# Residual sums by accumulating DMA, first squares on TensorE alone, and three smaller edits in a one-core streaming encoder layer

## The chip, the cores and the metric

The kernel runs on one core of a Trainium2 chip. The metric is the device time of one execution in microseconds (us). The engines are named as the profile names them: PE is TensorE (PEld its weight loads), DVE is VectorE, ACT is ScalarE, POOL is GpSimd, SP is SyncE, which here only issues DMAs.

## What is computed

One layer of a hybrid encoder, for 1024 prompt frames and 32 sample frames (T = 1056 tokens), with 1024 features and a feed-forward width of 2816, in float32:

```python
xn = rmsnorm(x, pre_mix_norm_w)
proj = xn @ w_in                                  # -> z | xbc | dt | u
y_ssd = ssd_mixer(z, xbc, dt_raw, ...)            # conv4, SiLU, chunked scan, 8 heads, gated norm
y_s5 = s5_mixer(u_s5, ...)                        # complex diagonal scan, GELU, GLU
mix = jnp.concatenate([y_ssd, y_s5], axis=-1) @ w_out
h = x + rmsnorm(mix, post_mix_norm_w)             # first residual sum
up, new_ffn = causal_dwconv(rmsnorm(h, pre_ffn_norm_w) @ w_up, ffn_hist, ffn_conv_w, ffn_conv_b)
gate, val = jnp.split(up, 2, axis=-1)
ffn = (jax.nn.gelu(gate, approximate=True) * val) @ w_down
y = h + rmsnorm(ffn, post_ffn_norm_w)             # second residual sum
```

## The kernel before

**Layout.** Everything is feature-major: 128 partitions by 8 feature blocks by tokens. The tokens are walked in three chunks, c0 of 512, c1 of 272 and c2 of 272 (block 0 is c0, block 1 is c1 and c2; the last 32 are the sample's). The matrix `o` (`O[b]`) holds the output projection and later h, `acc` (`ACC[b]`) the sum of the down projection.

**GEMMs.** Each product is three passes, high by high, low by high and high by low (L479). A weight tile `raw` of 512 KB is loaded by SP's DMA into a ring of two, its high part `wh` is copied by ACT (L535), its low part `wl` is subtracted by DVE (L713).

**Norms.** Squares (ACT) are added over pairs of feature blocks on POOL or DVE, a matmul with a column of ones (`ms<-onec`) brings the sum over features into a column, nine small DVE steps (L603 to L626) make 1/sqrt of it, `spread` puts the factors on a diagonal (`scr`, L646 and L647, or L639) and a matmul with ones spreads them over the partitions into PSUM (`ms<-scr,ones_r`). ACT then copies the factor to SBUF: `rbc` and `oacc` (r1 in the code), and `sacc` for the last norm.

**Stages in time.** Prologue (x loaded, split into `xh` by ACT and `xl` by DVE at L1045, squares, pair sums at L1029 on POOL); the input projections (u evacuated to `uext` at L758); the S5 scan and the SSD chunks beside them (masks `rh`, `rl` at L1349 on POOL, one pair for each SSD chunk); the output projection; `post` (from L1640), which scales `o` by r1 (L1659, DVE), adds x from the tile `xr` (L1660, POOL), splits h into `xh` and `xl`, adds its squares (L1666, POOL) and stores block 0's h to DRAM (`hd`, SP); the feed-forward blocks; `fin_out` and `apply`, which scale `acc` by the last factor (L1891, DVE or POOL by a table), add h (L1893, or L1896 from the reloaded `hr`) and store y (L1897, SP).

**What sets the order.** The side streams (S5, SSD, post, fin) are generators that are woven into the main GEMM stream. A planner then reads all instructions, finds their dependencies, prices each with a cost table (`cost`), makes a list schedule with a forward and a backward pass, and pins the order of every engine's queue. So an edit anywhere in the program, or in the table, can move instructions everywhere.

The two lines of `flush` on which the second edit turns:

```python
if k in (par["pairs"] if c == 0 else par["pairs2"]):
    G.tensor_tensor(a[-1], a[-1], r, add)
```

Of the kernel before, what the change touches and what calls it, by code (L numbers as in the profile page):

```python
# [9 lines left out]
F32 = mybir.dt.float32  # L10
# [9 lines left out]
WA = 512  # L20
# [161 lines left out]
class Plan:  # L182
# [61 lines left out]
    def read(self):  # L244
# [97 lines left out]
    def cost(self, q, i, ia, oa):  # L342
# [30 lines left out]
    def schedule(self, rank, pre, suc, forward=True, gate=None):  # L373
# [12 lines left out]
        while todo:  # L386
# [28 lines left out]
            if self.bytes[q]:  # L415
                if forward:
# [3 lines left out]
                end[q] = max(s + self.lat[q], wire + 0.8)  # L420
                lanes = lanes[1:] + [end[q]]
# [37 lines left out]
def body(tc, xT, wt, wdt, vec, cst, dtp, hist4, hist3, h0ssd, s5p, s5bc, s5d, glu, glub,  # L459
# [289 lines left out]
    h_dram = dram.tile([128, KD, WA], F32, name="hd")  # L749
# [591 lines left out]
    def ssd_front(c):  # L1341
# [301 lines left out]
    def post(b):  # L1643
        HN[b] = xtiles(b)
        for c in BLKC[b]:
# [7 lines left out]
            for j in range(4):  # L1653
                xr = iot("xr")[:, :, :w]
                D.dma_start(xr, xT[:, 2 * j:2 * j + 2, t0:t0 + w])
                for kk in range(2):
                    k = 2 * j + kk
                    h = O[b][:, k, o:o + w]
                    V.scalar_tensor_tensor(h, h, vc("post_mix", k), r1, mult, mult)  # L1659
                    (V if k in par["hv"] else G).tensor_tensor(h, h, xr[:, kk], add)  # L1660
# [9 lines left out]
                if b == 0:  # L1670
                    D.dma_start(h_dram[:, 2 * j:2 * j + 2], O[b][:, 2 * j:2 * j + 2, o:o + w])
# [188 lines left out]
    def fin_out(c):  # L1860
# [4 lines left out]
        r = fin[c][0]  # L1865
# [8 lines left out]
        if c == 1:  # L1874
            ap = [(1, j) for j in par["fp"][1]] + [(1, j) for j in range(4) if j not in par["fp"][1]][:par["ia"]]
        elif c == 2:
            ap = [(1, j) for j in range(4) if j not in par["fp"][1]][par["ia"]:] + ap
        with ExitStack() as es:
            if c == 2:
                es.enter_context(tc.issue_after(last[0].ins))  # L1880
            for c_, j in ap:
                apply(c_, j)
                yield 0.9

    def apply(c, j):
# [13 lines left out]
    hrs = {}  # L1899

    def fin_block(b):
        if b == 0:
            for j, n in enumerate(("ext0", "ext1", "W0", "G0", "T0", "C0")):
                h = tl(n, [128, 2 if j < 2 else 1, 512], "hr")
                k = 2 * j if j < 2 else j + 2
                D.dma_start(h, h_dram[:, k:k + h.shape[1]])
                for i in range(h.shape[1]):
                    hrs[k + i] = h[:, i]
# [37 lines left out]
```

## Time and profile before

| | us |
|---|---|
| median of three runs | 1296.92 |
| lowest and highest | 1296.79, 1300.04 |
| the profiled execution | 1294.34 |
| its span in the trace | 1292.4 |
| mean granted TensorE clock | 0.979 of 2.4 GHz |

The span is what the trace covers, from the first to the last recorded event; 1.94 us of the profiled execution lie outside it. The median lies 2.58 us above the profiled execution. Rows show a start and a length in us; an entry in brackets is the idle time of that engine before the row and what ended it. In rows by window the figure behind a busy time is the number of instructions.

### The profile page before, as it was taken

To read this page: it belongs to the slowest core of one execution; us is meant where nothing else is said; L and a number is where in the kernel's file an instruction comes from. 1 tells how busy PE (TensorE), PEld (TensorE's weight loads), DVE (VectorE), ACT (ScalarE), POOL (GpSimd) and SP (SyncE) were. 2 spreads that over 40 slices of the span, in tenths; PEclk is the share of its full clock that TensorE was granted. 3 is DMA by queue.
4 is the path that set the end of the run, shared out by engine and by line. 5 is a ranking of instruction groups with operands and counts; after the bars stand their busy time and mean duration, and the time that the engine had idled before them with its cause. 6 is when DMAs were issued, how large, how long until landed. Compare 5 with 4: busy or idle time off the path is not lost.

```text
span 1292.4 us, 20981 instructions
## 1 busy us (share of the span) xinstructions
PE 1225.8 (95%) x7880; PEld 1105.6 (86%) x7880; DVE 1035.2 (80%) x1781; ACT 574.5 (44%) x979; POOL 397.7 (31%) x577
## 2 busy tenths in 40 slices
PE   6879999999998999999999999998999999999995
PEld 5768888888877888878977888887999999999994
DVE  7898887988988998987688977679577777777777
ACT  7236466554555555543444433353523333333243
POOL 5364554544146433211345110015111111111113
PEclk8989999999998999999999999999999999999997
DMA  7133323233434423234433333222323332222212
GB/s 220 57 96 99 96 76 114 79 106 93 124 105 164 152 91 99 81 104 137 153 99 123 122 99 98 95 85 82 117 81 98 99 98 82 95 86 83 82 52 70
DMA packets 66901, 132.14 MB, mean 102 GB/s; under 512 B 13936, under 2 KB 34800, under 8 KB 66800
## 3 DMA queue, kind: packets, MB, share of 16 engines
q1 hardware_dynamic: 66800, 130.81, 32.2%
q8 instruction: 62, 1.02, 0.3%
q14 instruction: 39, 0.32, 0.1%
HBM read 111.69 MB, written 15.81 MB: 99 GB/s over the span
## 4 chain that ended last, share of the span: by engine, by line
PE 79%; DVE 10%; POOL 3%; issue 3%; DMA 2%; ACT 1%; SPq 1%; DVEq 0%; ACTq 0%; POOLq 0%
PE pm L479 70%; PE ms L479 9%; DVE wl L713 1%; POOL pacc L1666 1%; POOL o L1660 1%; DVE o L1659 1%; SPq L1122 1%; DMA xst<-xT 1%; DVE scr L647 1%; DVE scr L646 1%; POOL oacc L1628 1%; PE ms L483 1%; DVE pq L996 1%; POOL hq L1164 0%; DVE yr L1104 0%
## 5 line engine op out<-in xcount | busy, mean ns | idle before, releaser
L479 PE MATMUL pm<-xh,wh 128*128 128x272 f32 (+1 forms) x1616 | 532.1, 330 | 15.9 <-ACT wh L535 8.7
L479 PE MATMUL pm<-xh,wl 128*128 128x272 f32 (+1 forms) x1616 | 531.1, 329 | 7.4 <-DVE wl L713 7.3
L479 PE MATMUL pm<-xl,wh 128*128 128x272 f32 (+1 forms) x1616 | 529.8, 328 | 1.7 <-DVE xl L1045 1.7
L479 PEld LDWEIGHTS pm<-xh,wh 128*128 128x128 f32 x1616 | 309.9, 192 | 37.8 <-ACT wh L535 8.7
L479 PEld LDWEIGHTS pm<-xh,wl 128*128 128x128 f32 x1616 | 309.0, 191 | 30.8 <-DVE wl L713 9.1
L479 PEld LDWEIGHTS pm<-xl,wh 128*128 128x128 f32 x1616 | 309.9, 192 | 24.4 <-DVE xl L1045 3.0
L535 ACT ACTIVATE wh<-raw 128x1024 fp32r<-128x1024 f32 x120 | 126.9, 1057 | 177.5 <-PE pm L479 109.5
L713 DVE TENSOR_TENSOR wl<-raw,wh 128x1024 fp32r<-128x1024 f32 x120 | 154.9, 1291 | 26.6 <-ACT wh L535 26.1
L479 PE MATMUL pm<-al,dh 128*128 128x272 f32 (+1 forms) x528 | 171.4, 325 | 0.6 <-DVE al L1751 0.6
L479 PE MATMUL pm<-ah,dh 128*128 128x272 f32 (+1 forms) x528 | 171.7, 325 | 0.3 <-ACT ah L535 0.3
L479 PE MATMUL pm<-ah,dl 128*128 128x272 f32 (+1 forms) x528 | 170.8, 324 | 0.0
L1793 DVE TENSOR_TENSOR acc<-acc,pm 128x272 f32<-128x272 f32 (+1 forms) x235 | 121.1, 520 | 53.6 <-PE pm L479 52.5
L1738 DVE SCALAR_TENSOR_TENSOR ftmp<-fext,vec_t,ftmp 128x512 f32<-128x512 f32 (+1 forms) x176 | 143.1, 814 | 3.9 <-ACT ftmp L535 2.1
L1716 POOL COPY fext<-halo 128x2 f32<-128x2 f32 x88 | 33.6, 382 | 293.0 <-DVE ftmp L1738 271.5
L1721 DVE TENSOR_TENSOR fext<-pm,rbc 128x512 f32<-128x512 f32 (+2 forms) x132 | 67.5, 511 | 69.2 <-PE pm L479 65.8
L479 PEld LDWEIGHTS pm<-ah,dh 128*128 128x128 f32 x528 | 99.4, 188 | 8.6 <-ACT ah L535 0.7
L479 PEld LDWEIGHTS pm<-al,dh 128*128 128x128 f32 x528 | 99.3, 188 | 8.1 <-DVE al L1751 0.9
L479 PEld LDWEIGHTS pm<-ah,dl 128*128 128x128 f32 x528 | 99.2, 188 | 7.7 <-issue 0.3
L535 ACT ACTIVATE dh<-raw 128x1024 fp32r<-128x1024 f32 (+1 forms) x46 | 46.7, 1018 | 108.3 <-PE pm L479 96.8
L535 ACT ACTIVATE ftmp<-fext,vec_t 128x512 f32<-128x512 f32 (+1 forms) x88 | 72.3, 822 | 11.1 <-DVE fext L1721 5.7
L535 ACT ACTIVATE ftmp<-ftmp 128x512 f32<-128x512 f32 (+1 forms) x44 | 28.4, 644 | 87.0 <-DVE ftmp L1738 87.0
L1771 DVE TENSOR_TENSOR dl<-raw,dh 128x1024 fp32r<-128x1024 f32 (+1 forms) x46 | 55.9, 1216 | 13.6 <-ACT dh L535 13.6
(318 smaller groups left out, 1668.7 us busy)
## 6 DMA issues: line engine op xcount, KB each, us to landing
raw<-wt SPq DMA_DIRECT2D x164, 512.0 KB, 3.3
gluw<-glu SPq DMA_DIRECT2D x8, 512.0 KB, 3.4
xst<-xT SPq DMA_DIRECT2D x16, 136.0 KB, 3.3
pbd<-pbo SPq DMA_DIRECT2D x8, 272.0 KB, 2.6
xr<-xT SPq DMA_DIRECT2D x8, 272.0 KB, 3.2
pbi<-pbd SPq DMA_DIRECT2D x8, 272.0 KB, 3.5
yT<-acc SPq DMA_DIRECT2D x8, 272.0 KB, 2.3
ud<-uext SPq DMA_DIRECT2D x4, 528.0 KB, 4.0
```

What stands on the lines that cost most here:

```text
L479: PE.matmul(out, lhsT, rhs, start=start, stop=stop, **kw)
L483: PE.transpose(out, in_, ident)
L535: S.activation(out, in_, func, bias=bias, scale=scale)
L646: e.tensor_scalar(hi[:L, o:o + L], ident[:L, :L], r[:L, i:i + 1], None, mult)
L647: last[0] = V.scalar_tensor_tensor(lo[:L, o:o + L], ident[:L, :L], r[:L, i:i + 1], hi[:L, o:o + L].bitcast(F32), mult, sub)
L713: V.tensor_tensor(lo, r, hi.bitcast(F32), sub)
L996: V.tensor_scalar(pq[lo:hi, a], src[lo:hi, :, o:o + 8], sg, None, mult)
L1716: G.tensor_copy(e[:, 0:2], halo[:, j, :])
L1721: V.tensor_tensor(e[:, 2 + o:2 + o + wp], ps[:, :wp], rbc[:, t0:t0 + wp], mult)
L1738: V.scalar_tensor_tensor(t, e[:, i:i + n], vc("fw", 3 * j + i), t, mult, add)
L1771: V.tensor_tensor(l, rr, h.bitcast(F32), sub)
L1793: V.tensor_tensor(a, a, ps[:, :w], add)
```

## The change

Five edits, and a sixth in the planner's table.

1. **Residuals.** In `post`, x is no longer loaded into `xr` and added by POOL. POOL's queue issues a DMA from x in DRAM onto `o` that adds (`accum_op=add`), one for each two feature blocks. h is stored straight into the output `yT` by SP, for all chunks; `hd` and its reloads `hr` are gone. In `apply`, DVE alone multiplies, and POOL's queue issues a DMA that adds `acc` onto `yT` in DRAM. There are 12 + 12 such DMAs; 24 + 14 POOL steps, and the DVE steps L1893 and L1896, leave.
2. **First squares.** `pairs=()`: the five POOL sums of chunk 0's squares leave, and TensorE sums all eight (32 instead of 12 matmuls of one column before the factor of chunk 0).
3. **Masks.** Each SSD chunk's two POOL steps of 128x1024 with two tensor inputs become sixteen of 128x128 with one tensor input and a column as scalar.
4. **Last factor.** The ACT copy of the last factor to `sacc` is dropped; the multiplication reads PSUM.
5. **u.** `uext` is written in its own storage order, and PSUM and `rbc` are read with a stride, instead of the other way round.
6. **Planner.** POOL's DMAs are priced at 1.0 us of POOL and 3.5 us until landing, a GEMM matmul slightly differently, and two readers of a PSUM tile on one engine keep their order.

```diff
-pairs=(1, 2, 3, 5, 6)
+pairs=()
-            self.dur[q], self.lat[q] = 0.06, 2.0
+            self.dur[q], self.lat[q] = (0.06, 2.0) if e == "SP" else (1.0, 3.5)
-                d = max(0.43 * n + 6, 107 if m > 64 else 54)
+                d = max(0.426 * n + 9, 107 if m > 64 else 54)
...
-        V.tensor_tensor(ext4[j][:, :, n0:n1].rearrange("p s n -> p n s"),
-                        ps[:, :w].rearrange("p (n s) -> p n s", s=8),
-                        rbc[:, t0:t0 + w].rearrange("p (n s) -> p n s", s=8), mult)
+        V.tensor_tensor(ext4[j][:, :, n0:n1], ps[:, :w].rearrange("p (n s) -> p s n", s=8),
+                        rbc[:, t0:t0 + w].rearrange("p (n s) -> p s n", s=8), mult)
...
-            G.tensor_tensor(dst, src[:L, c].bitcast(F32)[:, :, None].to_broadcast([L, 8, L]), ub, mult)
+            for h in range(8):
+                G.tensor_scalar(dst[:, h, :], upper[:L, :L], src[:L, c, h:h + 1].bitcast(F32), None, mult)
...
-                D.dma_start(xr, xT[:, 2 * j:2 * j + 2, t0:t0 + w])
+                for kk in range(2):
+                    h = O[b][:, 2 * j + kk, o:o + w]
+                    V.scalar_tensor_tensor(h, h, vc("post_mix", 2 * j + kk), r1, mult, mult)
+                G.dma_start(O[b][:, 2 * j:2 * j + 2, o:o + w], xT[:, 2 * j:2 * j + 2, t0:t0 + w], accum_op=add)
...
-                    V.scalar_tensor_tensor(h, h, vc("post_mix", k), r1, mult, mult)
-                    (V if k in par["hv"] else G).tensor_tensor(h, h, xr[:, kk], add)
...
-                if b == 0:
-                    D.dma_start(h_dram[:, 2 * j:2 * j + 2], O[b][:, 2 * j:2 * j + 2, o:o + w])
+                D.dma_start(yT[:, 2 * j:2 * j + 2, t0:t0 + w], O[b][:, 2 * j:2 * j + 2, o:o + w])
...
-            act(r, norm_r(fin[c], w, scrt(*(("xo", "Z0"), ("xo", "W1"), ("T1", "G1"))[c]), G if c in par["fg"] else None, f"f{c}"),
-                AF.Copy)
+            fin[c] = [norm_r(fin[c], w, scrt(*(("xo", "Z0"), ("xo", "W1"), ("T1", "G1"))[c]), None, f"f{c}")]
...
-        e = G if j in par["fp"][c] else V
-        e.tensor_tensor(a, a, fin[c][0][:, None, :].to_broadcast([128, 2, w]), mult)
-        if b:
-            e.tensor_tensor(a, a, O[b][:, 2 * j:2 * j + 2, o:o + w], add)
-        else:
-            for kk in range(2):
-                e.tensor_tensor(a[:, kk], a[:, kk], hrs[2 * j + kk], add)
-        D.dma_start(yT[:, 2 * j:2 * j + 2, t0:t0 + w], a)
+        V.tensor_tensor(a, a, fin[c][0][:, None, :].to_broadcast([128, 2, w]), mult)
+        G.dma_start(yT[:, 2 * j:2 * j + 2, t0:t0 + w], a, accum_op=add)
```

**PE at the program's start.** `xh_111` and `xl_112` are the high and low part of chunk 0's x, `xh_165` and `xl_166` those of c1; `xst` is a tile of x that now holds its squares. Before, in the middle of the first GEMM rows:

```order
L479 MATMUL pm<-xh_111,wh 128x512
L479 MATMUL ms_295<-onec,xst 128x1
L479 MATMUL pm<-xh_165,wh 128x272
L479 MATMUL pm<-xl_112,wh 128x512
L479 MATMUL pm<-xh_111,wl 128x512
L479 MATMUL pm<-xl_166,wh 128x272
L479 MATMUL pm<-xh_165,wl 128x272
L479 MATMUL pm<-xh_165,wh 128x272
L479 MATMUL ms_295<-onec,xst 128x1 x11
```

After, from the first row of PE's queue:

```order
L1917 UNCONDITIONAL_BRANCH
L482 MATMUL ms_289<-onec,xst 128x1 x32
L482 MATMUL pm<-xh_110,wh 128x512
L482 MATMUL pm<-xl_111,wh 128x512
L482 MATMUL pm<-xh_110,wl 128x512
```

All sums of chunk 0's squares moved ahead of the first GEMM matmul; before, 22 GEMM matmuls stood ahead of the first of them. Ahead of the spread of chunk 0's factor (`ms<-scr,ones_r 128x512`) there stood 26 GEMM matmuls of 512 columns and 50 of 272, and now the 26 alone.

**POOL in post of block 0.** `o_3883` and `o_3953` are h of block 0, `pacc` the sum of its squares, `rh` and `rl` the masks of SSD chunks in work. Before:

```order
L1628 TENSOR_TENSOR oacc<-oacc,osq 128x512 x3
L1349 TENSOR_TENSOR rl_4719<-dtal,cst_t 128x1024
L1660 TENSOR_TENSOR o_3883<-o_3883,xr 128x512 x4
L1666 TENSOR_TENSOR pacc<-pacc,xr 128x512 x2
L1660 TENSOR_TENSOR o_3883<-o_3883,xr 128x512 x2
L1666 TENSOR_TENSOR pacc<-pacc,xr 128x512 x2
L1660 TENSOR_TENSOR o_3883<-o_3883,xr 128x512 x2
L1666 TENSOR_TENSOR pacc<-pacc,xr 128x512 x2
L1349 TENSOR_TENSOR rh_4718<-dtah,cst_t 128x1024
```

After:

```order
L1629 TENSOR_TENSOR oacc<-oacc,osq 128x512 x3
L1659 DMA o_3953<-xT 128x2x512 x4
L1668 TENSOR_TENSOR pacc<-pacc,xr 128x512 x4
L1350 TENSOR_SCALAR rl_4795<-cst_t,dtal 128x128
L1668 TENSOR_TENSOR pacc<-pacc,xr 128x512 x2
L1350 TENSOR_SCALAR rh_4794<-cst_t,dtah 128x128 x7
L1350 TENSOR_SCALAR rl_4795<-cst_t,dtal 128x128 x7
L1350 TENSOR_SCALAR rh_4794<-cst_t,dtah 128x128
```

The eight sums L1660 became four DMA issues, which stand together ahead of the sums of squares; mask steps went behind them. On PE, 126 GEMM matmuls of 272 columns stand between the spread of r1 and the column sums of `pacc` in the changed kernel.

**DVE at the program's end.** `acc_8887` and `acc_8990` are block 1's sum, `ms_13110` and `ms_13247` the last factors of c1 and c2 in PSUM. Before, the last rows:

```order
L639 TENSOR_TENSOR scr<-cst_t,nry 128x384
L1891 TENSOR_TENSOR acc_8887<-acc_8887,sacc 128x2x272
L1893 TENSOR_TENSOR acc_8887<-acc_8887,o_6230 128x2x272
L1891 TENSOR_TENSOR acc_8887<-acc_8887,sacc 128x2x272
L1893 TENSOR_TENSOR acc_8887<-acc_8887,o_6230 128x2x272
L1891 TENSOR_TENSOR acc_8887<-acc_8887,sacc 128x2x272
L1893 TENSOR_TENSOR acc_8887<-acc_8887,o_6230 128x2x272
L1891 TENSOR_TENSOR acc_8887<-acc_8887,sacc 128x2x272
L1893 TENSOR_TENSOR acc_8887<-acc_8887,o_6230 128x2x272
L1940 UNCONDITIONAL_BRANCH
```

After:

```order
L1882 TENSOR_TENSOR acc_8990<-acc_8990,ms_13110 128x2x272
L1794 TENSOR_TENSOR acc_8990<-acc_8990,pm 128x272
L1858 TENSOR_TENSOR sacc<-sacc,osq 128x272
L1882 TENSOR_TENSOR acc_8990<-acc_8990,ms_13110 128x2x272 x3
L606 TENSOR_SCALAR nrt<-ms_13223 128x2
...
L642 TENSOR_TENSOR scr<-cst_t,nry 128x384
L1882 TENSOR_TENSOR acc_8990<-acc_8990,ms_13247 128x2x272 x4
L1917 UNCONDITIONAL_BRANCH
```

The four pairs of multiplication and addition became four multiplications, and c1's four stand ahead of the last factor's arithmetic. POOL's queue ends with eight rows of `L1883 DMA yT<-acc_8990 128x2x272`, where before it ended with two multiplications and two additions.

## Rows read from the trace of the kernel before

**Rows 1.** The page: busy time, share of the span and instructions of each engine.

```profile
PE 1225.8 (95%) x7880; PEld 1105.6 (86%) x7880; DVE 1035.2 (80%) x1781; ACT 574.5 (44%) x979; POOL 397.7 (31%) x577
```

**Rows 2.** Windows: length; busy PE, PEld, DVE, ACT, POOL; clock; DMA share; GB/s.

```profile
100.00:380.00 280.00, 266.95 (x1805) 239.88 (x1804) 239.85 (x396) 156.16 (x329) 120.46 (x119) 0.99 0.34 98
...
640.00:720.00 80.00, 76.43 (x391) 62.40 (x390) 66.66 (x137) 35.70 (x67) 38.93 (x45) 1.00 0.39 120
...
910.00:1260.00 350.00, 350.00 (x2793) 350.00 (x2792) 252.47 (x461) 125.17 (x183) 44.56 (x155) 1.00 0.26 86
1260.00:1292.40 32.40, 16.51 (x128) 15.35 (x127) 23.98 (x52) 10.65 (x26) 12.02 (x9) 0.73 0.20 70
```

**Rows 3.** Timeline of the prologue: start, length, engine, line, tiles, [idle before].

```profile
4.24 1.28 ACT L535 ACT_TABLE_LOAD   x1 [4.24 <-DMA xst<-xT]
...
8.70 0.79 PE L479 MATMUL pm<-xh,wh 128*128 128x512 f32 x1 [8.70 <-ACT wh L535]
...
18.87 0.63 ACT L535 ACTIVATE xst<-xst 128x512 f32<-128x512 f32 x1 [0.40 <-DVE xl L1045]
...
27.50 0.28 DVE L646 TENSOR_SCALAR scr<-cst_t,nry 128x128 fp32r<-128x128 f32 x1
...
29.08 10.03 POOL L1029 TENSOR_TENSOR xst<-xst 128x272 f32<-128x272 f32 x9 [2.52 <-ACT xst L535]
...
36.25 1.21 PE L479 MATMUL ms<-onec,xst 128*128 128x1 f32 x12 [0.78 <-ACT rbc L535]
...
38.21 1.08 DVE L758 TENSOR_TENSOR uext<-pm,rbc 128x512 f32<-128x512 f32 x1
```

**Rows 4.** Groups by form: count, busy us, mean ns, idle before; L1716: ns min/median/max.

```profile
L758 DVE TENSOR_TENSOR uext<-pm,rbc 128x512 f32<-128x512 f32 x4 | 4.3, 1084 | 0.0
...
L1349 POOL TENSOR_TENSOR rh<-dtah,cst_t 128x1024 fp32r<-128x1024 f32 x8 | 16.6, 2074 | 18.0 <-DVE R L1162 11.1 <-PE ms L479 6.9
...
L1716 POOL COPY fext<-halo x88: 180/185/1049, 357.4 to 1239.0; 128x2 f32<-128x2 f32 x88
...
L535 ACT ACT_TABLE_LOAD x18 | 23.1, 1283 | 10.6 <-DVE yr L900 6.1 <-DMA xst<-xT 4.2
```

**Rows 5.** Timeline of post of block 0.

```profile
401.77 9.92 DVE L1659 SCALAR_TENSOR_TENSOR o<-o,vec_t,oacc 128x512 f32<-128x512 f32 x7 [1.22 <-ACT oacc L535]
...
413.94 0.39 PE L479 MATMUL pm<-xh,wl 128*128 128x272 f32 x1 [4.23 <-DVE wl L713]
```

**Rows 6.** The end of block 0 (fin0): timeline, then a window.

```profile
890.62 4.49 DVE L1896 TENSOR_TENSOR acc<-acc,hr 128x512 f32<-128x512 f32 x2
...
900.63 0.57 PE L479 MATMUL pm<-xh,wh 128*128 128x272 f32 x1 [4.12 <-DVE fext L1721]
...
898.00:906.00 8.00, 4.40 (x18) 4.11 (x19) 7.97 (x7) 0.75 (x2) 7.92 (x7) 0.57 0.34 131
```

**Rows 7.** Timeline of the tail, after the last GEMM matmul.

```profile
1273.19 0.44 DVE L1793 TENSOR_TENSOR acc<-acc,pm 128x272 f32<-128x272 f32 x1 [0.77 <-PE pm L479]
...
1276.83 0.20 DVE L603 TENSOR_SCALAR nrt<-ms 128x2 f32<-128x2 f32 x2
1277.07 1.05 DVE L606 TENSOR_SCALAR nry<-nrt 128x3 int32<-128x3 int32 x1
...
1278.35 1.18 DVE L621 SCALAR_TENSOR_TENSOR nra<-nra,nrt 128x3 f32<-128x3 f32 x1
1279.56 0.16 DVE L622 SCALAR_TENSOR_TENSOR nry<-nra,nry 128x3 f32<-128x3 f32 x1
...
1282.89 0.72 DVE L1891 TENSOR_TENSOR acc<-acc,sacc 128x544 f32<-128x544 f32 x1 [0.40 <-ACT sacc L535]
1282.94 1.87 POOL L1891 TENSOR_TENSOR acc<-acc,sacc 128x544 f32<-128x544 f32 x1 [3.43 <-ACT sacc L535]
```

**Rows 8.** Tile yT: SP's issues (ns min/median/max), and issue to landing.

```profile
L1897 SPq DMA_DIRECT2D yT<-acc x12: 372/378/462, 896.3 to 1289.3; - x12
...
DMA to landing us min/median/max: 2.2/2.5/5.4
```

More of the change, by code (lines that the diff above doesn't have):

```diff
@@ L48 @@
            run3=0.5, uload=6.619, swap_pool=1, z_s5=1, ssd0=13.784, ssd1=0.0, ssd2=2.778, gate0=76.032, glu0=0.384, glu1=2.807, abufs=2,
-           cvat='run7', tcat=1, late_at=2, nsq=1, fg=(), fp=((1, 3), (1, 3), (3,)), fch=(0, (0, 1), 2), pfin=0, q0=0, q1=0, q2=0, nb=0,
+           cvat='run7', tcat=1, late_at=2, nsq=1, fg=(), fp=((), (), ()), fch=(0, (0, 1), 2), pfin=0, q0=0, q1=0, q2=0, nb=0,
            hv=(), av=(3,), post0=0.802, dn_at=((3, 0), (3, 1)), ob_at=22, sa=2, sb=1, y5b=0, cvb=2.11, msb=(1, 1, 2, 2, 2), pch0=(3,),
-           pch1=(3,), pch2=(3, 4), pf=0, pb=500, pg=0, pn=500, pr=0, pairs=(1, 2, 3, 5, 6), cf=4, cb=1, cg=0, cf2=2, cb2=(0, 1), cg2=0,
+           pch1=(3,), pch2=(3, 4), pf=0, pb=500, pg=0, pn=500, pr=0, pairs=(), cf=4, cb=1, cg=0, cf2=2, cb2=(0, 1), cg2=0,
            pgt=500, p5at=1, ng=0, n12=(2, 0), cho=2, dtlag=112.5, ng2=1, pairs2=(1, 2, 3, 5, 6, 7))
@@ L276, in read @@
             for _, g in ia:
+                if g[0].startswith(("ms", "pm")):
+                    self.pre[q].update(k for k, h in r.get(g[0], ()) if self.eng[k] == self.eng[q])
                 r.setdefault(g[0], []).append((q, g))
@@ L415, in schedule @@
             if self.bytes[q]:
-                if forward:
+                if forward and e == "SP":
                     s = max(s, lanes[0])
@@ L419, in schedule @@
                 wire = max(wire, s + 0.9) + self.bytes[q] / 280e3
-                end[q] = max(s + self.lat[q], wire + 0.8)
-                lanes = lanes[1:] + [end[q]]
+                end[q] = max(s + self.dur[q] + self.lat[q], wire + 0.8)
+                if e == "SP":
+                    lanes = lanes[1:] + [end[q]]
             else:
@@ L748, in body @@
     pb_dram = dram.tile([128, KD, T - WA], F32, name="pbd")
-    h_dram = dram.tile([128, KD, WA], F32, name="hd")
     ext4 = {}
@@ L1346, in ssd_front @@
         rl = sst([128, 8, 128], f"rl{b}", dt=F32R)[:L, :, :L]
-        ub = upper[:L, None, :L].to_broadcast([L, 8, L])
         for dst, src in ((rh, DT["ah"]), (rl, DT["al"])):
-            G.tensor_tensor(dst, src[:L, c].bitcast(F32)[:, :, None].to_broadcast([L, 8, L]), ub, mult)
+            for h in range(8):
+                G.tensor_scalar(dst[:, h, :], upper[:L, :L], src[:L, c, h:h + 1].bitcast(F32), None, mult)
         psx = mst()
@@ L1864, in fin_out @@
         yield 3
-        r = fin[c][0]
         with tc.high_priority(par["pn"]):
-            act(r, norm_r(fin[c], w, scrt(*(("xo", "Z0"), ("xo", "W1"), ("T1", "G1"))[c]), G if c in par["fg"] else None, f"f{c}"),
-                AF.Copy)
+            fin[c] = [norm_r(fin[c], w, scrt(*(("xo", "Z0"), ("xo", "W1"), ("T1", "G1"))[c]), None, f"f{c}")]
         yield 1
@@ L1873, in fin_out @@
         ap = [(c, j) for j in range(4)]
[L1874 to L1883, printed above, removed]
+        for c_, j in ap:
+            apply(c_, j)
+            yield 0.9
     def apply(c, j):
@@ L1889, in apply @@
         a = ACC[b][:, 2 * j:2 * j + 2, o:o + w]
-        e = G if j in par["fp"][c] else V
-        e.tensor_tensor(a, a, fin[c][0][:, None, :].to_broadcast([128, 2, w]), mult)
-        if b:
-            e.tensor_tensor(a, a, O[b][:, 2 * j:2 * j + 2, o:o + w], add)
-        else:
-            for kk in range(2):
-                e.tensor_tensor(a[:, kk], a[:, kk], hrs[2 * j + kk], add)
-        D.dma_start(yT[:, 2 * j:2 * j + 2, t0:t0 + w], a)
-    hrs = {}
-    def fin_block(b):
[L1902 to L1908, printed above, removed]
+        V.tensor_tensor(a, a, fin[c][0][:, None, :].to_broadcast([128, 2, w]), mult)
+        G.dma_start(yT[:, 2 * j:2 * j + 2, t0:t0 + w], a, accum_op=add)
+    def fin_block(b):
         for c in BLKC[b]:
```

## The prediction

> **What bounds the kernel now.** I read the busy totals first: PE is busy for 1225.8 us of the span of 1292.4 [rows 1], so at most 67 us of idle PE time are there to be won. The windows by stage say where they lie. From 910 to 1260 PE is busy without a gap, 2793 matmuls in 350 us, or 0.125 us for one of 272 columns [rows 2]; an engine that gets faster there gives nothing. From 100 to 380 PE lacks 13.05 us, from 640 to 720 it lacks 3.57, and in the tail 15.9 of 32.4 [rows 2]. So the edits are worth what they do at the prologue, in the S5 and SSD stage, around the two posts, at the end of block 0 and in the tail, and each is priced there.
>
> The timelines of those places show one pattern: DVE and POOL lengthen each other. A DVE step on three columns takes 0.16 us, but 1.05 and 1.18 beside POOL [rows 7]; adding `hr` takes 2.25 us a step (4.49 / 2) beside POOL's multiplication [rows 6]. The change takes many POOL steps away, so it works on the price of others' steps too.
>
> **The change part by part.** The sums go against the profiled execution, 1294.34 us, of which 1292.4 are the span.
>
> *Prologue.* Before, PE starts its GEMM at 8.70, the last square of chunk 0 is done at 18.87 + 0.63 = 19.5, and the first `uext` is written at 38.21 [rows 3]. Chunk 0's factor can't be spread earlier since POOL's sums, the column sums and slowed diagonal steps stand ahead of it; the GEMM goes on behind at 36.25 + 1.21 = 37.5, with 26 matmuls of 512 columns and 50 of 272 done. Now ACT does 16 steps of 0.63 from 4.24 + 1.28 = 5.5, where its table load ends [rows 3], so the squares end near 15.6; `wh` follows, so PE starts its GEMM near 16.7, 8 us later than before. Its 26 matmuls of 512 columns (0.125 x 512 / 272 = 0.235 us each) take 6.1 us, to 22.8. DVE's `wl`, seven `xl` steps of c1, nine small steps (0.16 [rows 7]) and eight diagonal ones (0.28 [rows 3]) stand between the squares and the spread and end near 26.3, an estimate in which no step is lengthened; after the spread (0.5) the 50 matmuls of 272 columns take 6.3 us, so PE is by 33.5 where it was at 37.5: **-4 us**. The 20 more one-column matmuls at 1.21 / 12 = 0.10 us [rows 3] stand where PE has nothing else. The lower end: the factor is ready at 24, -6.5. The upper: POOL's twelve remaining sums (10.03 us [rows 3]) slow DVE as before and the GEMM starts at a low clock (the tail's window shows 0.73 where PE idles [rows 2]), +2. Contiguous writing can take at most part of 1.08 us for each of four steps [rows 4], on DVE beside PE's work; counted at nothing, as DVE's cover is there (239.85 us busy in 280 [rows 2]).
>
> *S5 and SSD stage.* ACT's queue holds 28 table loads for 18, ten more at 1.283 us [rows 4], 12.8 us, since the new order alternates functions more often. Nine of the ten stand in the S5 part. ACT is busy 156 of 280 us there [rows 2], which covers most; but S5 chains pass through ACT. Masks: two steps of 2.07 us per SSD chunk [rows 4] become 16 of 128 elements a row. The nearest row of small POOL steps is the copy of two elements, 0.185 us in the median and 1.049 at most [rows 4]: 3.0 to 16.8 us for 4.1. I take 0.3, the median plus a little for the length, so 4.8 us a chunk, on an engine that is busy 120 of 280 us [rows 2]: nothing. The stage gets **+4 us**, a third of the table loads. Its ends are +12.8 (all of them on the path) and -3 (fewer collisions between DVE and POOL shorten a few of the 13 us of gaps).
>
> The Trainium skill, "GPSIMD Engine Reference", section "Engine selection", calls POOL roughly at line rate for one-input steps and about half of VectorE's speed for two-input ones; by it the masks would gain, not lose. No row here shows such a step.
>
> *Post of block 0.* PE waits 4.23 us for `wl` [rows 5], which stands in DVE's queue among the seven L1659 steps that take 9.92 us, 1.42 each [rows 5]. POOL's eight sums go, so these steps fall towards 0.72 (as the tail's steps of 544 columns, alone [rows 7]); DVE gains about 5 us ahead of `wl`. In their place comes the landing of a DMA between `o` and `xh`. POOL's issue isn't shown anywhere before, as no DMA is POOL's. It lies between 0.37 us (SP's issue [rows 8]) and 1.87 (a POOL step on such a tile [rows 7]); I take 1.0, near the middle. Landing lies between 2.2 and 5.4 [rows 8]; I take 3.5, a little over the median of 2.5, for the added read. Then h is complete 8 x 0.72 + 1 + 3.5 = 10.3 us after r1, and 126 matmuls of 272 columns, 15.7 us, stand in PE's queue between r1 and the sums of `pacc`: covered by 5 us. SP's stores of h wait for these landings where `hd` waited for POOL; one or two weight loads stand behind each, in a ring two deep. **-4 us** (from -4.2 to +2, when issue and landing are both at their upper ends).
>
> *Post of block 1.* The same with 8 shorter DMAs; the stage lacks 3.57 us [rows 2]: **-1** (from -3 to +2).
>
> *End of block 0.* In the window 898 to 906 PE does 18 matmuls in 8 us, where 64 fit at 0.125: 5.75 us lost, behind `fext` in DVE's queue, which stands behind additions of 2.25 us [rows 6]. These additions and POOL's multiplications go, four multiplications of DVE stay, spread out among the GEMM's steps: **-5** (from -5.75 to +2).
>
> *Tail.* From 1273.19 to the end it is 19.2 us [rows 2, 7]. It falls into: up to the factor's arithmetic at 1276.83, 3.64; from there to the first multiplication at 1282.89, 6.06; from there to the end, 9.5 [rows 7]. The first stays (the squares set it). The second loses 1.05 + 1.18 - 2 x 0.16 = 1.9, as POOL is silent: 4.15. The third becomes four multiplications of 0.72, one issue of 1.0 and a landing of 3.5: 7.4. The sum is 15.2, **-4 us**. The lower end, with ACT's copy saved in the second part (0.7), a DVE step less in the first (1.0), issue 0.37 and landing 2.2: -7.6. The upper: issue 1.87 and landing 5.4 in a queue of eight, +2.
>
> By the Trainium skill, "DMA: Bandwidth & Descriptors", section "Anatomy of one DMA — SWDGE (gpsimd) path", a DMA from this queue takes about 2.0 us plus its bytes over 436 GB/s, which for 278 KB is an estimate of 2.6 us; by it the tail would be 0.9 us shorter. No row of before shows such a DMA.
>
> The sum is -4 + 4 - 4 - 1 - 5 - 4 = -14: 1280.3 us against the profiled execution. The median lies 2.6 us above that, so **1283 us**. Taking the terms' distances to their ends as independent, the root of the sum of squares is 8.5 us downwards and 15.5 upwards.
>
> **The rivals.**
>
> *The new order eats it.* The planner has re-priced every GEMM matmul and pinned all queues anew. If the ten table loads fall on the path (+8.8 over my term) and the prologue's lead is lost to the later GEMM start (+4), the time is 1283 + 12.8 = 1296: no change. For it: nine of ten loads stand in one stage that has PE gaps. Against it: ACT is busy little more than half of that stage. Chance 0.13.
>
> *POOL is held by each DMA: slower.* The place is the tail. The last eight DMAs stand in one queue, from about 0.8 us behind the last GEMM sum; they end at 0.8 + 8t + 3.5, t being POOL's time for one. At t = 1.9 us this is the 19.2 us of before. If POOL writes the descriptors row by row, or waits until earlier ones are consumed, t could be 5 us, the longest landing [rows 8]: 44.3 us, 29 more than I forecast, **1312 us**, with little more from the posts. For it: no row shows POOL's issue, and the bounds above are other work's. Against it: SP's issue of such a tile takes 0.37 us [rows 8]. Chance 0.12.
>
> The Trainium skill, "SBUF — State Buffer", section "SBUF: two separate sides", names a way to this rival: POOL can't write descriptors while certain VectorE steps hold the ports that they share. No row here shows it.
>
> *Collisions move rather than vanish.* POOL's issues slow DVE as its sums did: half of the posts', block 0's and the tail's gains stay, +7.5: 1290. Faster still. Chance 0.13.
>
> *More than forecast.* S5 stage, prologue and tail at their lower ends (-7, -2.5, -3.6): 1270. Chance 0.05.
>
> **How the numbers follow.** My forecast has the rest, 0.57, with a range of its own of 1274 to 1293. The range for 8 in 10 takes in the best case and the case of no change: 1270 to 1298; only the slower rival lies outside, and the edges of the others. About 0.3%, or 3.9 us, is what a measurement here can tell from no change: 1293.0 to 1300.8 is "same". Faster: 0.57 + 0.05 + 0.12 of the moved collisions = 0.74. Same: 0.13 + 0.01 = 0.14. Slower: 0.12.
>
> **What would show it.** In the changed kernel's timeline: first `uext` near 30 us and PE's second start by 27; no PE wait over 1 us for `wl` near 410; no window with half-idle PE near 900; 15 us from the last GEMM sum to the end; POOL's DMA rows of 1 us. I am wrong if POOL's rows for these DMAs last 2 us or more, if the landings exceed 5 us, or if PE's idle time between 100 and 380 grows by over 8 us.

## The result and the profile after

The changed kernel takes **1385.32 us** (median; 1384.09 to 1387.33), the kernel before 1298.48 in the same comparison: 1.0668 times as long, 95% interval 1.0643 to 1.0694, or 87 us slower. I had forecast 1283, with 1270 to 1298 as the range. The profiled execution took 1384.09 us, its span is 1382.3. The page's busy totals, in the columns of [rows 1]:

```profile
PE 1258.3 (91%) x7920; PEld 1132.6 (82%) x7920; DVE 981.9 (71%) x1777; ACT 585.1 (42%) x986; POOL 419.0 (30%) x686
```

DVE has 53 us less to do, as intended, and POOL 21 us more, though all its residual sums are gone. PE is busy 33 us longer, with 40 more records of one-column matmuls, and idle for 124 us instead of 67. Where that lies shows when the two traces are cut at the same events. Each number but the last is the start of a row that exists in both:

| event | before | after | lost since the event above |
|---|---|---|---|
| first write of `uext` | 38.2 | 35.1 | -3.1 |
| first S5 scan (`R`, DVE) | 101.3 | 100.4 | +2.2 |
| last S5 scan | 272.2 | 290.0 | +18.7 |
| first scaled `o` of post, block 0 | 401.8 | 432.9 | +13.3 |
| first `fext` (FFN of block 0) | 437.9 | 487.4 | +18.4 |
| first multiplication by the last factor, c0 | 889.4 | 961.4 | +22.5 |
| last sum of the GEMM, block 1 | 1273.2 | 1341.4 | -3.8 |
| end of the span | 1292.4 | 1382.3 | +21.7 |

The windows between some of these events, in the columns of [rows 2]:

```profile
100.40:290.00 189.60, 171.66 (x1132) 157.73 (x1130) 153.15 (x255) 108.09 (x237) 82.18 (x93) 0.95 0.31 88
...
432.90:487.40 54.50, 37.84 (x204) 35.06 (x202) 22.16 (x39) 19.17 (x37) 26.29 (x27) 0.72 0.61 156
...
703.30:815.00 111.70, 94.20 (x424) 76.83 (x423) 78.48 (x167) 40.75 (x70) 26.61 (x40) 0.89 0.43 109
...
961.00:1341.40 380.40, 378.83 (x3017) 377.83 (x3016) 275.86 (x512) 140.44 (x213) 53.12 (x172) 1.00 0.29 88
1341.40:1382.30 40.90, 3.00 (x20) 2.12 (x20) 7.29 (x21) 0.99 (x3) 9.74 (x8) 0.53 0.47 54
```

Post of block 0 in the kernel before, between the same events:

```profile
401.80:437.90 36.10, 31.87 (x224) 29.73 (x223) 35.17 (x37) 20.77 (x38) 28.84 (x16) 0.95 0.52 179
```

Post of block 0 (432.9 to 487.4) leaves PE idle for 16.7 us (4.2 before), and the mean granted clock of the stretch, between TensorE's levels of 1.2 and 2.4 GHz, is 0.72 for 0.95: 204 matmuls keep PE busy for 37.8 us, where 224 took 31.9. The tail has doubled, though PE, DVE and ACT are done by 1350.4.

POOL's timeline of the tail, with DVE's last row in it, shows why (x4 are four instructions; in brackets the idle time before and its releaser, where "issue" means that the engine waited for nothing that the profile shows):

```profile
1341.90 1.21 POOL L1883 DMA_DIRECT2D yT<-acc  x1 [2.38 <-DVE acc L1794]
1346.65 1.22 POOL L1883 DMA_DIRECT2D yT<-acc  x1 [3.54 <-DVE scr L642]
1347.76 2.61 DVE L1882 TENSOR_TENSOR acc<-acc,ms 128x544 f32<-128x544 f32 x4 [1.37 <-PE ms L482]
...
1351.65 1.21 POOL L1883 DMA_DIRECT2D yT<-acc  x1 [3.77 <-issue]
...
1375.99 1.22 POOL L1883 DMA_DIRECT2D yT<-acc  x1 [3.78 <-issue]
```

An accumulating DMA costs POOL 1.22 us, near the 1.0 that I took. But the next one starts 4.87 us later (eight issues, (1375.99 - 1341.90) / 7), though its data is there: DVE's last multiplication ends at 1350.4. Landing takes 4.4 to 4.9 us, 4.6 in the median, and every issue from the second on starts 0.3 us after the DMA before it has landed. The same stands in post of block 0, whose DMAs of 512 KB land after 6.4 to 8.1 us:

```profile
434.63 1.39 POOL L1659 DMA_DIRECT2D o<-xT  x1 [12.39 <-DVE o L1658]
...
441.93 1.25 POOL L1659 DMA_DIRECT2D o<-xT  x1 [5.91 <-issue]
450.27 1.22 POOL L1659 DMA_DIRECT2D o<-xT  x1 [7.10 <-issue]
456.97 1.23 POOL L1659 DMA_DIRECT2D o<-xT  x1 [5.47 <-issue]
```

There the work behind it waits too. From the waits of ACT and of PE in the whole program (us in total, times, longest):

```profile
ACT xr L538 <- DMA o<-xT: 29.8, 7, 6.6
...
PE ms L482 <- POOL pacc L1668: 19.6, 3, 9.5
PE pm L482 <- ACT pbo L538: 13.6, 3, 6.8
```

ACT's squares of h (`xr`) wait for the landing, ACT's copies of GEMM results (`pbo`) stand behind them in its queue, and PE waits for a free PSUM tile. All 13.6 us of this last wait lie in post of block 0. Of the 19.6 us that PE waits for the sums of squares (`pacc`) 17.5 lie in post of block 1.

The second surprise is the masks, to be held against [rows 4] (groups by form: count, busy, mean ns):

```profile
L1350 POOL TENSOR_SCALAR rh<-cst_t,dtah 128x128 fp32r<-128x128 f32 x64 | 53.5, 851 | 10.5 <-DVE R L1163 9.8 <-DVE o L1623 0.7
L1350 POOL TENSOR_SCALAR rl<-cst_t,dtal 128x128 fp32r<-128x128 f32 x64 | 48.9, 779 | 18.4 <-DVE xl L1539 13.5 <-PE ms L482 4.9
```

102 us of POOL for what took 33 (16.6 for `rh` [rows 4] and as much for `rl`): sixteen steps of 0.8 us for two of 2.07.

### The profile page after: what moved, and what is told of

The parts are those of the page before. It is cut to its first block, busy times and chain, and to the rows that moved or that the text cites. A ratio compares the mean times of both kernels' runs of the same rounds, so it can differ in the third digit from the quotient of the medians.

```text
span 1382.3 us, 21149 instructions
## 1 busy us (share of the span) xinstructions
PE 1258.3 (91%) x7920; PEld 1132.6 (82%) x7920; DVE 981.9 (71%) x1777; ACT 585.1 (42%) x986; POOL 419.0 (30%) x686
## 4 chain that ended last, share of the span: by engine, by line
PE 62%; issue 4%; DMA 3%; POOL 3%; DVE 2%; ACT 1%; POOLq 0%; ACTq 0%; SPq 0%; DVEq 0%
PE pm L482 58%; PE ms L482 4%; DMA o<-xT 2%; POOL rh L1350 1%; POOL yT L1883 1%; POOL pacc L1668 0%; DMA yT<-acc 0%; DMA raw<-wt 0%; POOL oacc L1629 0%; ACT xh L538 0%; PE ms L486 0%; DMA z<-zd 0%; DVE scr L649 0%; DVE o L1658 0%; ACT wh L538 0%
## 5 line engine op out<-in xcount | busy, mean ns | idle before, releaser
L482 PE MATMUL pm<-xh,wh 128*128 128x272 f32 (+1 forms) x1616 | 535.0, 331 | 14.0 <-ACT pbo L538 13.6
L716 DVE TENSOR_TENSOR wl<-raw,wh 128x1024 fp32r<-128x1024 f32 x120 | 150.2, 1252 | 44.0 <-ACT wh L538 43.4
L1739 DVE SCALAR_TENSOR_TENSOR ftmp<-fext,vec_t,ftmp 128x512 f32<-128x512 f32 (+1 forms) x176 | 137.3, 780 | 15.8 <-ACT ftmp L538 13.3
L1734 POOL COPY o<-fext 128x2 f32<-128x2 f32 x44 | 10.2, 233 | 185.3 <-DVE fext L1722 185.3
```

The source lines that it names most:

```text
L482: PE.matmul(out, lhsT, rhs, start=start, stop=stop, **kw)
L716: V.tensor_tensor(lo, r, hi.bitcast(F32), sub)
L1734: G.tensor_copy(o3[:, j, 0, :], e[:, TP - WA:TP - WA + 2])
L1739: V.scalar_tensor_tensor(t, e[:, i:i + n], vc("fw", 3 * j + i), t, mult, add)
```

## The experiments

Theory after the result: four causes add up, namely (1) the space for the descriptors of POOL's DMAs (the program reserves 1024 bytes, `dynamic_dma_scratch_size`), which makes them wait for each other; (2) the small mask steps; (3) an order that the planner's new prices made worse; (4) the landing time in the posts. The rival to (1) is that accumulating DMAs never overlap; to (2) and (3), that each is the other's effect, since every edit reorders the whole program. Spans of two profiles differ by some us more or less than medians do: the profiled execution of before lies 4 us under the median of its runs. Two profiles of one order also differ: in b_evac, whose order is that of before, the first S5 scan starts at 104.3 for 101.3, but the last one 171.4 us after it for 170.9.

**ring1536.** The changed kernel with more descriptor space; no order changes.

```diff
-dynamic_dma_scratch_size=1024
+dynamic_dma_scratch_size=1536
```

> The changed kernel with 1536 instead of 1024 bytes of SBUF a partition for the descriptors of POOL's DMAs; every engine's order is the same. Theory (descriptor space): one such DMA fills over half of the space, so POOL waits about 3.6 us in front of each until the one before it has landed; with half as much again two fit, the eight issues of the tail go from 4.85 us apart to at most 2.5, the tail from 40.9 to about 25 us, the posts lose part of their waits too: 1350 to 1365 us. Rival (each accumulating DMA waits for the one before whatever the space): issues stay 4.85 us apart and the time stays at 1385.

1336.22 us, 49 less than the changed kernel (1.0296 times before, 1.026 to 1.0333). POOL in the tail:

```profile
1312.74 2.55 POOL L1883 DMA_DIRECT2D yT<-acc  x2 [2.38 <-DVE acc L1794]
...
1319.44 1.20 POOL L1883 DMA_DIRECT2D yT<-acc  x1 [0.87 <-issue]
...
1326.80 1.20 POOL L1883 DMA_DIRECT2D yT<-acc  x1 [1.38 <-issue]
1328.99 1.22 POOL L1883 DMA_DIRECT2D yT<-acc  x1 [0.99 <-issue]
```

The issues stand 2.32 us apart ((1328.99 - 1312.74) / 7), the first two follow each other directly, the tail is 22.8 us (1312.2 to 1335.0) for 40.9, post of block 0 41.9 (433.2 to 475.1) for 54.5. The gain was even larger than expected. The rival is out: with half as much space again, two DMAs are under way at a time, and where an issue waits it starts 0.3 us after the landing of the last DMA but one. The Trainium skill, "DMA: Bandwidth & Descriptors", section "SWDGE vs HWDGE vs iDMA", says that POOL appends such descriptors to rings in an SBUF carveout. The two kernels, which differ in that space alone, agree.

**halves.** The changed kernel, 1024 bytes, each accumulating DMA split in two of one feature block.

```diff
-        G.dma_start(yT[:, 2 * j:2 * j + 2, t0:t0 + w], a, accum_op=add)
+        for k in (2 * j, 2 * j + 1):
+            G.dma_start(yT[:, k:k + 1, t0:t0 + w], ACC[b][:, k:k + 1, o:o + w], accum_op=add)
```

> The changed kernel, 1024 bytes of descriptor space as there, with each accumulating DMA split in two of one feature block (24 + 24 for 12 + 12). Theory (the space is filled by descriptors, which a half-size DMA needs half as many of, so that two or three are under way at once): issues of the tail's sixteen 1.2 to 2.4 us apart, tail 25 to 38 us for 40.9, and the wait in front of each issue falls under 1.5 us. Rival (one DMA at a time whatever its size): sixteen issues at 4.4 us or more, tail 65 us or longer, 1415 us.

1352.84 us (1.0415, 1.0389 to 1.0442), 32 less than with whole ones. POOL in the tail, and the issues from there (KB each, median us to landing):

```profile
1338.37 2.67 POOL L1885 DMA_DIRECT2D yT<-acc  x3 [1.08 <-DVE acc L1883]
...
1346.86 0.86 POOL L1885 DMA_DIRECT2D yT<-acc  x1 [0.61 <-issue]
```

```profile
yT<-acc POOLq DMA_DIRECT2D x16, 136.0 KB, 3.5
```

An issue that follows a wait takes about 0.87 us, the sixteen start 1.28 us apart in the mean (1327.65 to 1346.86), three can be under way at once, and the tail is 22.2 us (1329.5 to 1351.7), less than I expected. More and smaller DMAs cured the tail with the space unchanged; post of block 0 still takes 49.4 us. So the limit goes not by the number of DMAs. Nor does it go by their bytes: in post of block 0 a half moves 256 KB, nearly as much as a whole DMA of the tail, and still three of them go out (441.1, 441.9, 442.4) before the fourth waits (445.55, 0.3 us after the first has landed). What fits is the number of packets: the trace has 272 for a whole DMA, 256 rows of 1088 or 2048 bytes and 16 small ones, and 144 for a half. The space of 1024 bytes held three halves (432 packets) and not two wholes (544).

**p_masks, pin_masks, masks_priced.** Edit 3 alone on the kernel before: with the planner free, with every queue's order pinned to that of before, and with the planner told a price of 0.6 us.

```diff
-            G.tensor_tensor(dst, src[:L, c].bitcast(F32)[:, :, None].to_broadcast([L, 8, L]), ub, mult)
+            for h in range(8):
+                G.tensor_scalar(dst[:, h, :], upper[:L, :L], src[:L, c, h:h + 1].bitcast(F32), None, mult)
```

> The kernel before with the masks as sixteen one-tensor steps, and the planner's rule for readers of PSUM, without which the order deadlocks (by itself the rule leaves every engine's order as it was). Theory (a small step of POOL costs 0.8 us, so a chunk's masks cost 13 us for 4.1 and POOL becomes late in the SSD stage): 1305 to 1315 us, most of it between the last S5 scan and the first sum of the output projection's squares. Rival (POOL's slack covers it, the SSD stage's loss came from the order): 1298, within 4 us.

> The kernel before with edit 3 alone and every engine's order pinned to that of before: each old mask step is replaced in its place by its eight small ones, nothing else moves. It parts what the masks cost themselves from what the new order costs, since of the 24 us that edit 3 cost with the planner free 15 arose before the last S5 scan. Theory (price): sixteen steps of 0.6 to 0.8 us for two of 2.05 make POOL late by about 9 us a chunk wherever a mask is awaited: 1306 to 1318 us, all of it after the last S5 scan, which stays near 272 to 276 us. Rival (order): the planner's new order made all of the loss, and pinned the time is 1298, within 4 us.

> The kernel before with edit 3 alone, and the planner told that a mask step of 128 elements takes 0.6 us on POOL (0.235 in its table). Theory (the S5 stage's loss of 15 us came from a planner that thought the masks free): last S5 scan back at 272 to 278, total as pinned or better, 1306 to 1314 us for 1322. Rival (any other order than the fitted one costs the S5 stage): last scan at 284 or later, 1318 to 1326.

Free: 1322.29 us (1.0192, 1.0157 to 1.0227), over my range of 1305 to 1315, with the last S5 scan at 287.1, 15 us later; I had placed most of the loss behind it. Pinned: 1316.01 (1.0147, 1.0116 to 1.0177), last scan at 272.5 as before. Told the price: 1317.94 (1.0156, 1.013 to 1.0182), last scan at 285.6. So the masks alone cost 17 us in the old order, all of it behind the scans, while POOL is busy with them for 94.8 us in place of 32.9. POOL of the pinned kernel ahead of post of block 0, and PE's wait there:

```profile
383.46 1.81 POOL L1642 TENSOR_TENSOR oacc<-oacc,osq 128x512 f32<-128x512 f32 x1 [0.74 <-ACT osq L549]
385.25 5.39 POOL L1362 TENSOR_SCALAR rl<-cst_t,dtal 128x128 fp32r<-128x128 f32 x8
390.60 1.28 POOL L1642 TENSOR_TENSOR oacc<-oacc,osq 128x512 f32<-128x512 f32 x1
391.86 5.68 POOL L1362 TENSOR_SCALAR rh<-cst_t,dtah 128x128 fp32r<-128x128 f32 x8
397.52 1.25 POOL L1642 TENSOR_TENSOR oacc<-oacc,osq 128x512 f32<-128x512 f32 x1
```

```profile
402.83 0.59 PE L493 MATMUL ms<-onec,oacc 128*128 128x1 f32 x2 [6.82 <-POOL oacc L1642]
```

Two masks of 5.4 and 5.7 us stand between sums that PE waits for; before, that wait was 1.5 us. The free order loses its time elsewhere, in the S5 stage, and the right price didn't bring that stage back: my theory on masks_priced fell. What in the new order delays the scans I didn't settle.

**b_plan.** Edit 6 alone; the instructions are those of before, only their order differs.

```diff
-                d = max(0.43 * n + 6, 107 if m > 64 else 54)
+                d = max(0.426 * n + 9, 107 if m > 64 else 54)
...
-                end[q] = max(s + self.lat[q], wire + 0.8)
+                end[q] = max(s + self.dur[q] + self.lat[q], wire + 0.8)
```

> The kernel before with edit 6 alone, the planner's prices and the rule for readers of PSUM; the program has 26 table loads on ACT for 18 and another order everywhere. Theory (the new prices make a worse order in the S5 stage, where 18.7 of the 87 us arose before any mask was made): 1310 to 1320 us, with the last S5 scan 15 to 20 us later. Rival (the S5 stage lost its time to the first squares and the other edits, the new prices alone do nothing): 1298, within 4 us.

1308.2 us (1.0079, 1.0048 to 1.0111), last S5 scan at 286.2. ACT's table loads in all (count, busy us, mean ns), and a wait of PE between 100 and 292 us:

```profile
L538 ACT ACT_TABLE_LOAD x26 | 33.4, 1283 | 6.9 <-DMA xst<-xT 4.5 <-DVE yr L903 2.0
```

```profile
PE ms L482 <- ACT ge L538: 6.5, 4, 2.2
```

The order alone costs 10 us, a little under what I expected. 14 are lost up to the last scan; 4 come back before post. The wait shown was 1.9 us in the kernel before. Table loads aren't needed for such a loss: from 100 to 292 us there are 13 of them here for 5 in the kernel before, 10 us of ACT, but p_masks, with 7, loses as much up to the last scan.

**p_pairs and b_evac.** Edit 2 alone (`pairs=()`), and edit 5 alone (the three lines of `evac_u`, as in the diff ahead).

> The kernel before with edit 2 alone (and the planner's rule for readers of PSUM, which by itself moves nothing); the planner orders anew, with 19 table loads. Theory (a lead at the start is lost in the S5 stage, whose own chain sets its length): the first u is written 2 to 4 us earlier, the first S5 scan starts at most 1 us earlier, total 1298 within 4 us. Rival (any new order costs the S5 stage about 15 us, since the parameters were fitted to the old one): last S5 scan at 285 or later, 1310 us.

> The kernel before with edit 5 alone, u written in its storage order; every engine's order is the same. Both theories expect little: each of the four 512-column steps falls from 1.08 to between 0.6 and 0.75 us, and the time stays at 1298 or falls by up to 2 us; a step that doesn't get shorter would refute that the stride of the write was the cost.

p_pairs: 1297.39 us (0.9993, 0.9972 to 1.0013); the first `uext` comes at 34.9, 3.3 earlier, but the first S5 scan at 102.2 for 101.3. Its last scan, at 274.2, shows that a new order need not delay the scans. b_evac: 1299.86 us (1.0009, 0.9991 to 1.0026). Its `uext` group:

```profile
L758 DVE TENSOR_TENSOR uext<-pm,rbc 128x512 f32<-128x512 f32 x4 | 4.5, 1117 | 0.0
```

1.12 us for 1.08 [rows 4]: moving the stride from the write to the reads doesn't shorten the step. What a stride costs at all isn't shown, as one is left in either form. Neither edit changes the time beyond its interval.

**post_dma.** The first residual alone by accumulating DMA, with 1536 bytes.

```diff
+                G.dma_start(O[b][:, 2 * j:2 * j + 2, o:o + w], xT[:, 2 * j:2 * j + 2, t0:t0 + w], accum_op=add)
...
-                    (V if k in par["hv"] else G).tensor_tensor(h, h, xr[:, kk], add)
```

> The kernel before with the first residual sum alone done by accumulating DMA, with 1536 bytes of descriptor space; h is stored and reloaded and the last residual added as before. Theory (a landing of 4.5 to 6 us stands between the scaled o and its split, on a path that PE waits for): the stage from the first scaled o to the first fext takes 40 to 43 us for 36.1, post of block 1 loses some us more, 1303 to 1310 us. Rival (the DMA is hidden and POOL's absence speeds DVE): 1290 to 1296.

1316.21 us (1.0134, 1.0116 to 1.0151): 17 us, above the range of the theory. POOL's issues in post of block 0, PE's waits in both posts, and the window of post of block 1, here and in the kernel before:

```profile
406.53 2.64 POOL L1661 DMA_DIRECT2D o<-xT  x2 [6.30 <-DVE o L1660]
413.05 1.22 POOL L1661 DMA_DIRECT2D o<-xT  x1 [3.88 <-issue]
416.30 1.20 POOL L1661 DMA_DIRECT2D o<-xT  x1 [2.02 <-issue]
```

```profile
430.28 2.85 PE L482 MATMUL ms<-onec,pacc 128*128 128x1 f32 x16 [3.01 <-POOL pacc L1670]
...
721.33 2.06 PE L482 MATMUL ms<-onec,pacc 128*128 128x1 f32 x12 [3.97 <-POOL pacc L1670]
```

```profile
640.00:780.00 140.00, 131.25 (x645) 110.24 (x644) 100.41 (x200) 55.90 (x93) 39.99 (x55) 0.94 0.42 115
...
640.00:780.00 140.00, 136.43 (x652) 111.56 (x651) 116.49 (x209) 58.25 (x94) 46.76 (x61) 1.00 0.35 110
```

From the first scaled `o` to the first `fext` it is 39.6 us for 36.1, just under the 40 to 43 expected. In the window of post of block 1 PE is idle for 8.75 us and its clock is 0.94, where before it was idle for 3.57 at 1.00: 5 us of idle time and up to 8 of clock (6% of 131), an estimate, of the 15 that are lost from the first `fext` to the first multiplication by the last factor. PE's waits for `pacc` are 11.7 us in the whole program, 2.3 before. So the landing sits on the path: the sums of squares of h come late, PE waits, and runs slower behind the wait. The order is new here too (22 table loads for 18, the last scan 2.2 us later), and no run with the old order pinned tells how much of the 17 us is its share.

**a_ring_oldmm_oldmasks.** The changed kernel with 1536 bytes, the old masks and the old price of a GEMM matmul.

> The changed kernel with 1536 bytes of descriptor space, the masks as before and the old price of a GEMM matmul in the planner; edits 1, 2, 4, 5 are left. Theory (the three costs found so far, descriptor space, masks and prices, make up the loss of 87, the rest is near nothing): 1298 to 1308 us, with the stage from the first scaled o to the first fext near 40 us (36 before) and a tail near 23 us. Rival (without them the gains that were forecast appear, 14 us of them): 1284.

1310.39 us (1.0104, 1.0074 to 1.0134); post of block 0 takes 41.6 us, the tail 22.8. This is 25.8 under ring1536, for masks and prices, and 11.6 over before. So the three causes make 75 of the 87 us; the rest isn't near nothing, as the theory had it, but 2 us over its upper end. It holds what the residuals by DMA still cost (post of block 0 is 5.5 us longer than before, the tail 3.6), what is left of the new order, and the gains of edit 4; no run parts these.

**k1 and k1_pairs_evac.** The kernel before with edit 4 and DVE doing all of the last residual (the ACT copy dropped, POOL's share and the order of tiles that belonged to it taken away, SP storing as before), and the same with edits 2 and 5.

```diff
+            fin[c] = [norm_r(fin[c], w, scrt(...), None, f"f{c}")]
...
-        e = G if j in par["fp"][c] else V
+        V.tensor_tensor(a, a, fin[c][0][:, None, :].to_broadcast([128, 2, w]), mult)
+        V.tensor_tensor(a, a, O[b][:, 2 * j:2 * j + 2, o:o + w], add)
```

> The kernel before with edit 4 alone and its consequence: the last factor is read from PSUM, DVE does all multiplications and additions of the last residual, SP stores as before; no accumulating DMA, POOL idle in the tail. Theory (the tail pays for collisions of DVE and POOL): tail 16 to 17 us for 19.2, the end of block 0 loses 2 us less, 1292 to 1295. Rival (DVE is the engine that sets the tail and takes POOL's share too): tail 19 us or longer, 1298 to 1302.

> The kernel before with edits 2, 4 and 5, no accumulating DMA, masks and prices as before. Theory (edit 4 alone gave 9 us, edits 2 and 5 alone nothing): 1286 to 1292 us, as edit 4 alone within its noise. Rival (the gains add, since edit 2 starts u 3 us earlier): 1283 to 1286.

k1: **1289.39 us** (0.9936, 0.991 to 0.9962), faster than both kernels and than I expected. With edits 2 and 5: 1289.63 (0.9928, 0.9908 to 0.9947), no more. DVE in k1's tail:

```profile
1274.18 0.43 DVE L1795 TENSOR_TENSOR acc<-acc,pm 128x272 f32<-128x272 f32 x1
...
1276.81 0.21 DVE L605 TENSOR_SCALAR nrt<-ms 128x2 f32<-128x2 f32 x2 [0.18 <-PE ms L481]
1277.06 0.17 DVE L608 TENSOR_SCALAR nry<-nrt 128x3 int32<-128x3 int32 x1
...
1278.64 0.56 DVE L641 TENSOR_TENSOR scr<-cst_t,nry 128x384 f32<-128x384 f32 x1
...
1280.56 0.72 DVE L1883 TENSOR_TENSOR acc<-acc,ms 128x544 f32<-128x544 f32 x1 [0.73 <-PE ms L481]
...
1285.49 0.72 DVE L1885 TENSOR_TENSOR acc<-acc,o 128x544 f32<-128x544 f32 x1
```

The small step takes 0.17 us for 1.05 [rows 7], no step is lengthened, and the tail is 15.2 us for 19.2, which was my forecast for the change, reached without its DMAs. From the first multiplication by the last factor to the last GEMM sum it is 381.1 us for 383.8. These two stages give 7 of the 9 us; where the rest arose the profiles don't show.

## Why the prediction was wrong

*Tail (-4; +21.7).* The step that failed is "one issue of 1.0 and a landing of 3.5": the sum gave the wait between two issues no term at all. It named it only in the rival (POOL held by each DMA), whose line 0.8 + 8t + 3.5 with the measured t of 4.87 gives 43.3; the tail is 40.9. The second of the rival's two mechanisms, a wait until earlier descriptors are consumed, was the right one, and its 0.12 was too little: nothing in the trace bore on t, since no DMA of before is POOL's, and the bounds that I set came from SP's issue and from an arithmetic step, whose rows show no such wait. My sign for it, POOL's rows of 2 us or more, would have missed it: the rows stay at 1.22, and the wait stands as idle time in front of them. Of the other parts the first two came out a little under the sum (2.6 us for 3.64, 3.75 for 4.15), and the landing, 4.6 for 3.5, over it. Even with 1536 bytes the tail is 22.8, eight issues being 2.32 us apart. That k1's tail is the 15.2 of my sum is chance: it has neither issue nor landing of POOL, but additions of DVE and stores of SP in their place.

*Post of block 0 (-4; +18.4) and of block 1 (-1; the most of +22.5).* The same missing wait made 12.6 of the 18.4 (54.5 against 41.9 in ring1536), and 14.7 of the 22.5 (474.0 us from the first `fext` to the first multiplication, against 459.3). The rest is the cover: I counted 10.3 us of chain, with one issue and one landing of 3.5, under 15.7 of matmuls. But the fourth DMA of block 0 went out at 456.97, 24 us after the first scaled `o`, a landing took 6.4 to 8.1 us there (4.6 to 6.0 in block 1), and ACT's queue carried the wait on to PE: the matmuls that were to cover it needed ACT's copies. DVE's scaling did fall as forecast, to 5.39 us for eight steps; it was no longer what PE waited for.

*S5 and SSD (+4; +18.7 and +13.3).* Two steps failed. The masks were given 0.3 us a step "on an engine that is busy 120 of 280 us: nothing". A step of 128 elements takes 0.60 in the median and 0.8 in the mean, inside my bounds. POOL's idle time hid most of the 62 us that this adds in pin_masks, but 17 us came through, in part as the wait of 6.8 us for a sum behind the masks; by the profiles 13.7 us are lost there between the last scan and post, near the 13.3 of the table. And the new order was priced by its table loads alone, at a third of 12.8 us; b_plan shows 10 us from order alone, 14 of loss up to the last scan, and p_masks loses as much there with two more loads for b_plan's eight. The two don't simply add, and which rows of the order delay the scans stays open.

The Trainium skill's rule that I put beside the masks ("GPSIMD Engine Reference", section "Engine selection", one-input steps near line rate) pointed further the wrong way, and the rows don't agree with it. The same step takes 0.35 us on 32 columns and 0.60 on 128, an estimate of 2.6 ns a column and 0.27 us for the step itself: eight steps make 4.8 us, some 2.2 for the steps and 2.6 for the columns, where one two-tensor step on all 1024 columns took 1.9 in the median.

*Prologue (-4; -0.9 at the first scan).* The first `uext` came 3.1 us earlier, where "near 30" would have been 8, and 65 us later most of the lead was gone; p_pairs shows the same (3.3 earlier, then 0.9 later at the first scan). The difference is no larger than the 3 us by which b_evac's first scan departs from that of before. What holds the first scan wasn't traced. The mechanism was right to the first event, and edit 2 alone was worth nothing in the time.

*End of block 0 (-5; -3.8).* Right: no window with half-idle PE stands near the first multiplications, and from there to the last GEMM sum it is 380.0 us for 383.8. k1, in which DVE keeps the additions and POOL's share is gone, has 381.1, so 2.7 of the 3.8 us need no DMA.

*The whole.* By medians the space makes 49.1 us (ring1536), masks and GEMM price together 25.8, and the rest 11.6, in all 86.5 of 87.

*The range.* It took the worst ends as independent and left the slower rival outside. With four terms resting on resources of which before has no row (a POOL DMA, a small POOL step of one tensor, a new order), the upper end had to reach the rival. Two slips of the working are too small to matter: the prologue's steps add up to 33.1, not 33.5, and half of the gains that the collisions take is 7, not 7.5.

## What to carry to other kernels

A DMA issued by GpSimd had a cost here that no arithmetic step shows: space for its descriptors. Look how much the program reserves and how many rows a DMA has; where only one fits, price a chain of n such DMAs as n landings, and give more space or make each DMA smaller. Splitting one step of an engine into eight multiplies its fixed cost, and an engine's idle share, though it may hide much, doesn't hide what stands in front of a step that another engine waits for. Where a planner orders everything, pin the old order and make the edit alone: that told the 17 us of the masks from the rest.

## What the runs showed of the hardware

- With 1024 bytes reserved, accumulating DMAs of 272 KB were issued 4.87 us apart, with 1536 bytes 2.32; halves of 136 KB, with 1024 bytes, went out 1.28 us apart in the mean (0.5 to 2.0). An issue that waited started about 0.3 us after a landing: that of the DMA one, two and three places ahead of it.
- Such an issue takes 1.22 us of POOL for 272 KB, 1.22 to 1.39 for 512 KB and 0.86 for 136 KB. Landing took 4.6 us in the median for 272 KB onto `yT`; SP's stores onto `yT` in the kernel before took 2.5 [rows 8]. The Trainium skill's fit ("DMA: Bandwidth & Descriptors", section "Anatomy of one DMA — SWDGE (gpsimd) path") gives an estimate of 2.6 us; here the measured 4.6, of DMAs that add, decides.
- A one-tensor POOL step of 128 elements took 0.60 us in the median; one of 32 took 0.35.
- TensorE's mean granted clock was 0.72 in the window of post of block 0, where it was idle for 16.7 of 54.5 us, and 0.95 before, with 4.2 of 36.1 idle: 204 matmuls took 37.8 us for 224 in 31.9. Here the waits cost more than their length.
